# Spatial gates: the first tile's z projection ahead of its u projection, and the block inverse's conversions in their written order on ScalarE

## The chip, the cores and the metric

The kernel runs on one core of a Trainium2 chip. A core has five engines that run side by side: TensorE (PE in the profile; its weight loads are PEld) for matmuls, VectorE (DVE), ScalarE (ACT) and GpSimd (POOL) for elementwise work, and SyncE (SP), which here only issues DMAs. ACT and POOL issue DMAs too. Each engine takes its instructions in the order in which they were queued; an instruction waits on semaphores for its inputs, and what is queued behind it waits as well.

The metric is the device time of one execution in microseconds. The kernel before takes 2145.91 us, the median of 3 runs (2145.07 to 2146.69).

## The reference

One layer of a backbone with three parallel token mixers, for 2048 sample tokens and 128 prompt tokens of width 1024:

```python
proj = jnp.einsum('btd,de->bte', xn, w_in)
qkv, beta, dec, z_a, u_b, v_b, z_b, x_c, z_c, gates = jnp.split(proj, points, axis=-1)
...
o, s_f, s_b = delta_bidir(q, k, v, g, beta, s0_f, s0_b)
o_a = (rmsnorm(o, o_norm_g) * jax.nn.silu(z_a)).reshape(B, T, W_BR)
o_b = chunk_sgu(u_b, v_b, sgu_norm_g, w_spatial, b_spatial) * jax.nn.silu(z_b)
o_c = fourier_mix(x_c, grid) * jax.nn.silu(z_c)
br = jnp.stack([o_a, o_b, o_c], axis=2)
pb = jnp.einsum('btnw,nwd->btnd', br, w_branch)
merged = jnp.einsum('btnd,btnd->btd', jax.nn.sigmoid(gates), pb)
return jnp.einsum('btd,de->bte', merged, w_out), s_f, s_b
```

Two parts matter here. `chunk_sgu` (branch B) normalizes v, mixes it over the 128 tokens of a chunk by `w_spatial`, giving vs, and multiplies u by it; the result is gated by silu(z). `delta_bidir` (branch A) is a gated delta rule: in each chunk of tokens a triangular system with a unit diagonal is solved, then a state is carried from chunk to chunk, forwards and backwards.

## The kernel before

The 2176 tokens lie along the free dimension as five tiles, `TBS`: four of 512 and one of 128. Every matmul operand is a pair of float16 tiles, a high and a low part, so a product of a weight block (8 contraction steps) with a tile of 512 tokens is 24 matmuls: high by high, high by low, low by high for each step (`gemm_T`, and the matmul itself is on line 250). A conversion of an array into such a pair is always an activation on ScalarE that writes the high part and an instruction on VectorE that subtracts it and writes the low part.

The program has a main line and a generator, `delta`, which is branch A's work. The main line runs the projections one after another: v for all 17 chunks (`spatial` mixes a chunk's v and makes `vs`, L1498; `vstore` writes it to DRAM, L1504), then the spatial gates (the loop `for g in range(4)` with tiles `ti` in it), then the Fourier branch, then the merges. After each product it calls `pace.tick(us)`, which takes one `weight_step` (a piece of the conversion of a later weight block: square on L315, scale, high part L327, low part L328) and advances `delta` by a step for each 1.6 us of its argument. The order in which all this is written gives the priorities.

The order on each engine is then made at build time: a planner runs through a simulated time and gives each engine the instruction of the best priority among those whose inputs it takes to be there. `tc.high_priority()` lifts an instruction above others. `tc.issue_after(ins)` forbids one to be queued ahead of `ins` on the same engine; it is no wait for its end. `queued()` of the wrapper `_InTurn` is that for the newest instruction written so far on the engine. On the chip the order is fixed.

*Spatial gates.* For each of the four column groups g the row `vrow` of vs is read back from DRAM into SBUF: for g = 0 in five pieces by SP (L1542), for later g in one read during the group before (L1548). For a tile, u is multiplied (24 matmuls into a PSUM bank of `ps_mm`, which has three), and L1554 on VectorE, of high priority, writes u times vs into `vrow`. Then `gate_unit` calls `silu_unit`: z is multiplied into another bank, ACT makes the sigmoid (L1454), VectorE z times it (L1456), both of high priority. `gate_unit` goes on with the product of the two on GpSimd (L1466), its squares on ACT (L1467) and the store to DRAM from GpSimd (L1468). `silu_unit` can also be called earlier and its result handed to `gate_unit` as `sg`; the Fourier branch does so for three tiles. In that case `gate_unit`'s own tick is 0.2 us and not that of a product.

*Branch A beside it.* `prep` prepares one chunk: TensorE transposes rows of k and q (L1016), ACT squares them (L1022), VectorE and GpSimd make the norms (L1023, L1024), VectorE writes `tok` (L1033), TensorE transposes it (L1049), ACT and VectorE make the pair `T` (L1050, L1051), products of T with itself follow (L1064 to L1069) and with q (L1080 to L1083). `late` issues the stores from ACT, one stage behind. `base_inverse` runs between the stages of `prep`, one step of it for each: for a group of up to four chunks it reads the blocks `nd` into the one buffer `XB` (L1103), turns a half of them (L1107), and in 31 rounds of a VectorE product (L1114) and a GpSimd subtraction (L1115) makes the inverse E. Then four conversions of E into `XB`, each of one activation (L1122) and one VectorE instruction (L1123), with a yield behind each, and stores of the result, which `late` issues from ACT (L1003) in the next stages. `XB` is read again for the next group when these stores have landed. When all chunks are done the last group's inverse runs, and then `scan`, which needs the results.

Of the kernel before, what the change touches and what calls it, by code (L numbers as in the profile page):

```python
# [14 lines left out]
AF = mybir.ActivationFunctionType  # L15
# [20 lines left out]
FS = 4096.0  # L36
# [158 lines left out]
def hybrid_flow_kernel(ctx: ExitStack, tc: tile.TileContext, x_prompt, x_sample, state_delta, c, c_ctx, w_ada,  # L195
# [4 lines left out]
    G, V, A, PE = [_InTurn(tc, e_) for e_ in (nc.gpsimd, nc.vector, nc.scalar, nc.tensor)]  # L200
    uid, rot = [0], [0]

    def nm(s):
        uid[0] += 1
        return f"{s}_{uid[0]}"
# [4 lines left out]
    def sb(pl, shape, tag, dt=F32, bufs=None):  # L210
        kw = {} if bufs is None else {"bufs": bufs}
        return pl.tile(list(shape), dt, tag=tag, name=nm(tag), **kw)
# [11 lines left out]
    def bank(pl, shape, tag="b"):  # L224
        if pl is ps_d:
            rot[0] += 1
            pl = ps_d[rot[0] % 3]
        return pl.tile(list(shape), F32, tag=tag, name=nm(tag))
# [110 lines left out]
    def gemm_T(ps, w, c0, rh, rl, nkt=KT, start=True, stop=True):  # L339
        for k in range(nkt):  # L340
            mm(ps, w.hi[:, k, c0:c0 + P], rh[:, k, :], start and k == 0, False)
            mm(ps, w.hi[:, k, c0:c0 + P], rl[:, k, :], False, False)
            mm(ps, w.lo[:, k, c0:c0 + P], rh[:, k, :], False, stop and k == nkt - 1)
            if k % 2:
                pace.part(rh.shape[-1] / 400)
# [57 lines left out]
    def getw(n=1, ahead=0):  # L403
        i = wnext[0]
        wnext[0] += n
        fetch(i + n)
        while len(wdone) - len(wsteps) < i + n:
            weight_step()
        fetch(i + n + ahead)
        r = wdone[i:i + n]  # L410
        return r[0] if n == 1 else r
# [34 lines left out]
    pace = Pace()  # L446
# [257 lines left out]
    for ti, (t0, tn) in enumerate(TBS):  # L704
        g = 0 if t0 < NS else 1
# [225 lines left out]
    for ct in range(12):  # L931
        w = getw(1, 2 if ct < 6 else min(4, 15 - ct))
# [159 lines left out]
    def base_inverse(g):  # L1092
        nt = len(GROUPS[g])
        nb = 16 * nt
        XB = sb(dq, [P, 2048], "XB")
        X, tmp = XB[:, 0:1024], XB[:, 1024:2048]
        E = sb(dq, [P, 1024], "E")
        if nt < 4:
            V.memset(X, 0.0)
            V.memset(tmp, 0.0)  # L1100
        b3 = lambda t_: t_.rearrange("p (j i) -> p j i", j=32)
        for d in range(2):
            SY.dma_start((X if d == 0 else tmp)[64 * d:64 * d + nb, :], ndD[g][d].rearrange("t h (b j) i -> (t h b) (j i)", b=4))  # L1103
        for _ in range(8):
            yield 0
        with V.queued():
            V.tensor_copy(b3(X[64:P, :]), tmp[64:P, :].rearrange("p (i j) -> p j i", j=32))  # L1107
        G.memset(E, 0.0)
        G.memset(E[:, 0:1024:33], 1.0)
        X3, E3 = b3(X), b3(E)  # L1110
        for k in range(31, 0, -1):
            n_ = 32 - k
            t3 = tmp[:, 0:k * n_].rearrange("p (j i) -> p j i", j=k)
            V.tensor_tensor(t3, X3[:, 0:k, k:k + 1].to_broadcast([P, k, n_]), E3[:, k:k + 1, k:32].to_broadcast([P, k, n_]), ALU.mult)  # L1114
            G.tensor_tensor(E3[:, 0:k, k:32], E3[:, 0:k, k:32], t3, ALU.subtract)  # L1115
            if k % 2 == 0:
                yield 1
        both = XB.bitcast(F16).rearrange("p (j l w c) -> p j l w c", j=32, l=2, w=2)
        for j0 in (0, 16):
            js = slice(j0, j0 + 16)  # L1120
            for w, src in ((0, E3), (1, E.rearrange("p (i j) -> p j i", j=32))):
                A.activation(both[:, js, 0, w, :], src[:, js], AF.Copy, scale=FS)  # L1122
                V.scalar_tensor_tensor(both[:, js, 1, w, :], src[:, js], FS, both[:, js, 0, w, :], ALU.mult, ALU.subtract)  # L1123
                yield 1
            out = [(eD[g][d][js].rearrange("j t (y x) -> (t y) j x", x=128),
                    both[64 * d:64 * d + nb, js].rearrange("p j l w c -> p j (l w c)")) for d in range(2)]
            if g < 4:
                extra.extend(out)
            else:
                SY.dma_start(*out[0])  # L1130
                A.dma_start(*out[1])
# [278 lines left out]
    def delta():  # L1410
# [5 lines left out]
        for i_, (g, ci, t) in enumerate(seq):  # L1416
            if ci == 0 and g:
                for r_ in base:
                    if r_:
                        yield 1  # L1420
                base = base_inverse(g - 1)
            for n_, _ in enumerate(prep(g, ci, t, seq[i_ + 1][2] if i_ < 16 else None, held)):
                yield 1
                if next(base, 0):
                    yield 1
# [6 lines left out]
        for _ in base_inverse(4):  # L1432
            yield 1
# [14 lines left out]
    def silu_unit(ti, w, out_scale=None):  # L1448
        t0, tn = TBS[ti]
        ps = bank(ps_mm, [P, tn])  # L1450
        gemm_T(ps, w, 0, xh[:, :, t0:t0 + tn], xl[:, :, t0:t0 + tn])
        sg = sb(ep, [P, tn], "sg", bufs=4)
        with tc.high_priority():
            A.activation(sg, ps, AF.Sigmoid, scale=w.inv)  # L1454
        with tc.high_priority():
            V.scalar_tensor_tensor(sg, ps, w.inv if out_scale is None else out_scale, sg, ALU.mult, ALU.mult)  # L1456
        return sg

    def gate_unit(n, g, ti, w, src, sg=None, out_scale=None):

        t0, tn = TBS[ti]
        own = sg is None
        if own:
            sg = silu_unit(ti, w, out_scale)
        o = sb(ep, [P, tn], "st", bufs=3)
        G.tensor_tensor(o, sg, src, ALU.mult)  # L1466
        A.activation(sg, o, AF.Square, accum_out=oss[n][:, g * 5 + ti:g * 5 + ti + 1])  # L1467
        G.dma_start(obD[n][g, :, t0:t0 + tn], o)  # L1468
        pace.tick(tn / 100 if own else 0.2)
# [73 lines left out]
    for g in range(4):  # L1543
        uw, zw = getw(2, 2)
        vrow = vnext
        if g < 3:
            vnext = sb(vp, [P, NTOK], "vrow")
            SY.dma_start(vnext, vsD[g + 1])  # L1548
        for ti, (t0, tn) in enumerate(TBS):
            st = vrow[:, t0:t0 + tn]  # L1550
            ps = bank(ps_mm, [P, tn])
            gemm_T(ps, uw, 0, xh[:, :, t0:t0 + tn], xl[:, :, t0:t0 + tn])
            with tc.high_priority():
                V.scalar_tensor_tensor(st, ps, uw.inv, st, ALU.mult, ALU.mult)  # L1554
            pace.tick(tn / 100)
            gate_unit(1, g, ti, zw, st)

    vst.close()

# [18 lines left out]
    for g in range(4):  # L1578
        xw, zw = getw(2, 2)
# [611 lines left out]
```

## Time and profile before

| what | before |
| --- | --- |
| median of 3 runs | 2145.91 us |
| the profiled execution's own time | 2150.07 us |
| its span in the profile | 2148.3 us |
| mean granted TensorE clock | 0.992 |
| busy: TensorE, VectorE, ScalarE, GpSimd | 2085.2, 1327.9, 1060.8, 843.3 us |
| L1554, u times vs | 20 times, 13.3 us |
| L1454, sigmoid of the gates of both branches | 40 times, 24.8 us |
| L1456 in the spatial gates | 20 times, 13.3 us |
| L1122, high parts of the inverse | 20 times, 15.6 us |
| L1123, low parts of the inverse | 20 times, 18.1 us |
| HBM traffic | 186 GB/s over the span |

A line of the profile's order of time reads: start in us, duration, engine, line of the kernel, operation, output and inputs with their shapes, how many in a row, and in brackets how long the engine sat idle before and what ended that. A matmul of 512 columns is shown with 0.38 us, but the next begins 0.215 us later, since they are pipelined. The granted clock is a share of the full speed. An idle time that is put down to one releaser can have had another: the profile names the input that came last by its records.

### The profile page before, as it was taken

The numbers are of one execution on the slowest core, as the hardware profiler recorded it, in microseconds if no ns is written. First come the engines' busy times: TensorE is split into PE (matmuls) and PEld (weight loads), VectorE is DVE, ScalarE is ACT, GpSimd is POOL, SyncE is SP. The second block draws the span as 40 slices with busy tenths as digits, with TensorE's granted clock in tenths as the row PEclk, the third lists the DMA queues.
The fourth block names the chain that finished last, engine by engine and source line by source line (L and its number), as shares of the span: only waits on it lengthen the run. The fifth ranks groups of instructions, "written<-read, shape, count | busy, mean of one in ns | idle before, by whom it ended". The sixth has DMA issues, their size and how long they took to land.

```text
span 2148.3 us, 42630 instructions
## 1 busy us (share of the span) xinstructions
PE 2085.2 (97%) x16133; PEld 1196.8 (56%) x16133; DVE 1327.9 (62%) x2945; ACT 1060.8 (49%) x2457; POOL 843.3 (39%) x1089
## 2 busy tenths in 40 slices
PE   7999999999999999989899999999999999999997
PEld 4454444455555677777555556565655444444443
DVE  6656854388777786456655555766665564666245
ACT  5554744475656664445544445665653353453112
POOL 0321332225565555542321233354542234333464
PEclk9999999999999999999999999999999999999999
DMA  9525722277877743444655555867664655456852
GB/s 353 219 77 189 267 102 102 74 223 226 259 228 246 225 138 93 121 132 138 205 182 161 167 162 184 258 206 232 210 204 127 209 167 173 167 198 240 335 220 89
DMA packets 222910, 403.25 MB, mean 188 GB/s; under 512 B 39720, under 2 KB 109632, under 8 KB 219888
## 3 DMA queue, kind: packets, MB, share of 16 engines
q1 hardware_dynamic: 167664, 290.84, 42.5%
q0 software_dynamic: 15216, 65.89, 8.2%
q10 hardware_dynamic: 39824, 43.79, 6.0%
q8 instruction: 127, 2.08, 0.4%
q14 instruction: 79, 0.65, 0.1%
HBM read 258.19 MB, written 142.24 MB: 186 GB/s over the span
## 4 chain that ended last, share of the span: by engine, by line
PE 70%; DVE 9%; DMA 9%; ACT 4%; POOL 4%; issue 3%; SPq 1%; ACTq 0%; DVEq 0%; POOLq 0%
PE b L250 66%; PE b L182 4%; DMA st<-br 2%; POOL E L1115 1%; DMA pa<-pa 1%; DMA wst<-in_w_blk_dram 1%; DVE XB L1114 1%; POOL st L1466 1%; DMA ab<-in_w_adb_dram 1%; PE b L1016 1%; DMA sqk<-qk 1%; DMA ei<-XB 0%; ACT xh L182 0%; ACT nd L1066 0%; DVE XB L1123 0%
## 5 line engine op out<-in xcount | busy, mean ns | idle before, releaser
L250 PE MATMUL b<-xh,whi 128*128 128x512 f16 (+1 forms) x1920 | 651.1, 348 | 2.8 <-DVE sg L1456 1.8
L250 PE MATMUL b<-xl,whi 128*128 128x512 f16 (+1 forms) x1920 | 651.2, 348 | 0.0
L250 PE MATMUL b<-xh,wlo 128*128 128x512 f16 (+1 forms) x1920 | 650.1, 347 | 0.0
L250 PEld LDWEIGHTS <-whi 128*128 128x128 f16 x3856 | 352.7, 98 | 326.4 <-issue 7.3
L250 PEld LDWEIGHTS <-wlo 128*128 128x128 f16 x1928 | 188.8, 98 | 176.1 <-issue 2.2
L250 PE MATMUL b<-big,bhi 128*128 128x512 f16 (+1 forms) x960 | 252.3, 347 | 1.9 <-ACT big L1699 1.1
L250 PE MATMUL b<-big,blo 128*128 128x512 f16 (+1 forms) x480 | 163.1, 347 | 0.0
L1743 POOL TENSOR_TENSOR mrow<-mrow,sg 128x512 f32<-128x512 f32 (+1 forms) x80 | 94.4, 1182 | 131.2 <-DVE sg L1742 99.5
L953 POOL TENSOR_TENSOR cy<-cy,raw 128x545 f32<-128x545 f32 (+1 forms) x48 | 65.8, 1395 | 181.8 <-ACT raw L952 181.8
L250 PEld LDWEIGHTS <-xh 128*128 128x128 f16 x1496 | 116.9, 98 | 28.8 <-issue 1.4
L250 PEld LDWEIGHTS <-bhi 128*128 128x128 f16 x960 | 87.7, 98 | 78.1 <-issue 2.6
L1115 POOL TENSOR_TENSOR E<-E,XB 128x31 f32<-128x31 f32 (+15 forms) x155 | 94.1, 607 | 85.7 <-DVE XB L1114 68.8
L250 PEld LDWEIGHTS <-xl 128*128 128x128 f16 x1068 | 98.1, 98 | 44.8 <-DMA tw<-tw 1.4
L1733 ACT ACTIVATE sg<-b,winv 128x512 f32<-128x512 f32 (+1 forms) x120 | 73.9, 616 | 87.1 <-PE b L250 86.4
L1188 POOL COPY T<-ES 32x256 f16<-32x256 f16 x68 | 31.8, 467 | 188.6 <-DMA ES<-ei 167.9
L250 PE MATMUL b<-whi,xh 128*128 128x128 f16 x544 | 92.8, 219 | 0.0
L250 PE MATMUL b<-whi,xl 128*128 128x128 f16 x544 | 92.8, 219 | 0.0
L250 PE MATMUL b<-wlo,xh 128*128 128x128 f16 x544 | 92.8, 219 | 0.0
L328 DVE SCALAR_TENSOR_TENSOR wlo<-wst,wsc,whi 128x1024 f16<-128x1024 f32 x52 | 71.1, 1368 | 33.1 <-ACT whi L327 32.7
L315 ACT ACTIVATE wlo<-wst 128x1024 f16<-128x1024 f32 x52 | 54.9, 1055 | 54.5 <-DMA wst<-in_w_blk_dram 51.2
L1114 DVE TENSOR_TENSOR XB<-XB,E 128x31 f32<-128x31 f32 (+15 forms) x155 | 55.2, 356 | 41.8 <-POOL E L1115 41.2
L1295 POOL TENSOR_TENSOR skn<-skn,ed 128x512 f32<-128x512 f32 x34 | 37.7, 1109 | 109.7 <-DMA skn<-kv 109.7
(532 smaller groups left out, 4317.9 us busy)
## 6 DMA issues: line engine op xcount, KB each, us to landing
wst<-in_w_blk_dram SPq DMA_DIRECT2D x58, 512.0 KB, 4.5
pa<-pa POOLq DMA_DIRECT2D x16, 896.0 KB, 4.4
qkv<-cy POOLq DMA_DIRECT2D x12, 1089.0 KB, 5.3
st<-br SPq DMA_DIRECT2D x48, 256.0 KB, 3.2
mrow<-mrg SPq DMA_DIRECT2D x16, 576.0 KB, 4.6
pa<-pa SPq DMA_DIRECT2D x5, 1792.0 KB, 17.3
dc<-dec SPq DMA_DIRECT2D x17, 512.0 KB, 4.8
kq<-qkv SPq DMA_DIRECT2D x34, 256.0 KB, 4.5
```

The costliest lines, as they stand in the source:

```text
L182: self.last = f(*args, **kw)
L250: newest[0] = PE.matmul(out, l, r, start=start, stop=stop, skip_group_check=reopened)
L315: w.squared = A.activation(w.lo, st, AF.Square, accum_out=ss)
L328: w.low = V.scalar_tensor_tensor(w.lo, st, s, w.hi, ALU.mult, ALU.subtract)
L953: G.tensor_tensor(y[:, c0:c1], y[:, c0:c1], raw[:, 1 + c0:1 + c1], ALU.mult)
L1016: PE.transpose(ps[:, hs(h)], cur[part][:, h, :], ident)
L1114: V.tensor_tensor(t3, X3[:, 0:k, k:k + 1].to_broadcast([P, k, n_]), E3[:, k:k + 1, k:32].to_broadcast([P, k, n_]), ALU.mult)
L1115: G.tensor_tensor(E3[:, 0:k, k:32], E3[:, 0:k, k:32], t3, ALU.subtract)
L1188: G.tensor_copy(T16[rows(a0, b), :, :, b], ES[0:32, :, 2 * a0 + b, :, wT])
L1295: G.tensor_tensor(h3(kn_), h3(kn_), bc(ed[:, d, t, :], P), ALU.mult)
L1733: gated_[0] = A.activation(sg, ps, AF.Sigmoid, scale=gw.inv)
L1743: G.tensor_tensor(mr, mr, sg, ALU.add)
```

## The change

Two edits. In the spatial gates, for the first tile of the first group alone, z is multiplied, its sigmoid taken and a tick made before u is multiplied; `gate_unit` gets the result and makes its short tick. The tile so has three ticks and not two: 5.12, 5.12 and 0.2 us. In the block inverse each of the four high-part activations may no longer be queued on ScalarE ahead of the newest instruction that was written for ScalarE before it.

```diff
             for w, src in ((0, E3), (1, E.rearrange("p (i j) -> p j i", j=32))):
-                A.activation(both[:, js, 0, w, :], src[:, js], AF.Copy, scale=FS)
+                with A.queued():
+                    A.activation(both[:, js, 0, w, :], src[:, js], AF.Copy, scale=FS)
                 V.scalar_tensor_tensor(both[:, js, 1, w, :], src[:, js], FS, both[:, js, 0, w, :], ALU.mult, ALU.subtract)
                 yield 1
...
             st = vrow[:, t0:t0 + tn]
+            front = None
+            if (g, ti) == (0, 0):
+                front = silu_unit(ti, zw)
+                pace.tick(tn / 100)
             ps = bank(ps_mm, [P, tn])
             gemm_T(ps, uw, 0, xh[:, :, t0:t0 + tn], xl[:, :, t0:t0 + tn])
             with tc.high_priority():
                 V.scalar_tensor_tensor(st, ps, uw.inv, st, ALU.mult, ALU.mult)
             pace.tick(tn / 100)
-            gate_unit(1, g, ti, zw, st)
+            gate_unit(1, g, ti, zw, st, front)
```

## The prediction

> **What bounds the kernel now.** First the head of the page and its chain of waits: which engine is full, and what the end hangs on.
>
> ```profile
> span 2148.3 us, 42630 instructions
> PE 2085.2 (97%) x16133; PEld 1196.8 (56%) x16133; DVE 1327.9 (62%) x2945; ACT 1060.8 (49%) x2457; POOL 843.3 (39%) x1089
> ...
> PE 70%; DVE 9%; DMA 9%; ACT 4%; POOL 4%; issue 3%; SPq 1%; ACTq 0%; DVEq 0%; POOLq 0%
> ```
>
> TensorE is busy for 2085.2 of 2148.3 us. Neither edit takes a matmul away, so nothing can be won but idle time of TensorE, 63.1 us in the whole span. Second, the busy time by stretch, to see how much of it lies where the diff works. The columns are the stretch and its length, busy time with instruction counts of TensorE, of its weight loads, of DVE, ACT and POOL, then the granted clock, the DMA share and GB/s.
>
> ```profile
> 541.00:575.00 34.00, 31.61 (x180) 16.32 (x179) 23.24 (x52) 19.59 (x63) 15.77 (x25) 1.00 0.87 286
> 575.00:640.00 65.00, 63.23 (x441) 36.45 (x439) 50.53 (x114) 40.02 (x123) 43.92 (x62) 1.00 0.70 222
> 640.00:750.00 110.00, 110.00 (x830) 66.51 (x829) 79.38 (x182) 68.08 (x209) 61.68 (x88) 1.00 0.74 236
> ...
> 890.00:930.00 40.00, 33.58 (x345) 22.81 (x343) 16.25 (x41) 15.02 (x36) 20.00 (x34) 0.87 0.45 134
> ```
>
> The spatial gates run from about 527 to 750 us. Their start leaves TensorE idle for 34.00 - 31.61 = 2.39 us, the next 65 us for 1.77 us, the rest for nothing. The gap of 890 to 930 us (6.42 us, and a clock of 0.87) is where the scan begins. Third, the order of time around the first tile, engine by engine: start, duration, engine, line, operation, and in brackets the idle time before it with what ended it. ACTq and SPq are the DMA issues of ACT and SP.
>
> ```profile
> 541.59 1.12 DVE L1498 SCALAR_TENSOR_TENSOR vs<-b,vg,bsp 128x128 f32<-128x128 f32 x4
> ...
> 542.74 0.38 ACTq L1504 DMA_DIRECT2D vs<-vs  x1
> ...
> 543.16 0.69 ACT L1454 ACTIVATE sg<-b,winv 128x512 f32<-128x512 f32 x1 [4.29 <-DVE wsc L278]
> ...
> 543.88 0.75 DVE L1456 SCALAR_TENSOR_TENSOR sg<-b,winv,sg 128x512 f32<-128x512 f32 x1
> ...
> 546.76 1.04 POOL L1024 TENSOR_TENSOR ss<-ss,mhalf 128x4 f32<-128x4 f32 x1
> ...
> 547.56 0.17 DVE L1023 TENSOR_SCALAR ss<-ss 128x4 f32<-128x4 f32 x1 [0.53 <-ACT sq L1022]
> ...
> 548.57 2.23 SPq L1542 DMA_DIRECT2D vrow<-vs  x5
> ...
> 551.17 0.75 DVE L1554 SCALAR_TENSOR_TENSOR vrow<-b,winv,vrow 128x512 f32<-128x512 f32 x1 [3.44 <-DMA vrow<-vs]
> ...
> 551.83 0.68 DVE L1033 TENSOR_TENSOR tok<-b,ss 128x512 f32<-128x512 f32 x1
> ...
> 552.43 2.39 DVE L1123 SCALAR_TENSOR_TENSOR XB<-E,XB 128x512 f16<-128x512 f32 x2
> ...
> 552.66 0.63 PE L1049 MATMUL b<-cst,tok 128*128 128x128 f32 x4 [1.85 <-DVE tok L1033]
> ...
> 557.43 0.60 ACT L1050 ACTIVATE T<-b 128x512 f16<-128x512 f32 x1 [3.36 <-DVE XB L1123]
> ...
> 558.81 0.77 PE L250 MATMUL b<-T 128*128 128x128 f16 x11 [0.17 <-DVE T L1051]
> ...
> 569.34 0.63 PE L1049 MATMUL b<-cst,tok 128*128 128x128 f32 x4 [0.33 <-DVE tok L1033]
> ...
> 586.78 0.38 PE L250 MATMUL b<-xh,whi 128*128 128x512 f16 x1 [1.77 <-DVE sg L1456]
> ```
>
> The first tile's u product (L1554) needs vrow, which goes through DRAM: DVE ends the last vs at 542.71, ACT stores it from 542.74, SP can start reading it back only at 548.57, and DVE gets it at 551.17. DVE takes its queue in order, so it idles 3.44 us before L1554. Behind it stands L1033, whose own input was there when L1024 ended, at 546.76 + 1.04 = 547.80. TensorE stands in its turn before the transposes L1049 of tok, 1.85 us. That wait, 0.17 and 0.33 us make 2.35 of the 2.39 us.
>
> **The change, part by part. First, z ahead of u.** The 24 matmuls of each product are the same and only change places. They end here, the first row the last of the first product and the second that of the second:
>
> ```profile
> 533.69 0.38 PE L250 MATMUL b<-xh,wlo 128*128 128x512 f16 x1
> ...
> 540.21 0.38 PE L250 MATMUL b<-xh,wlo 128*128 128x512 f16 x1
> ```
>
> So z is complete at about 534.1 instead of 540.6 us, and u at 540.6 instead of 534.1. The u product has to wait for vrow until 551.17 either way, so being 6.5 us later costs it nothing: 551.17 - 540.6 leaves 10.6 us of cover. Its PSUM bank was held until 551.9 before, and that stays; z's bank was free at 544.6 and is free earlier.
>
> What moves is the sigmoid (0.69) on ACT and its product (0.75) on DVE. They leave the places at 543.16 and 543.88 and enter at about 534 to 536, among the work that makes the last vs:
>
> ```profile
> 534.22 0.63 ACT L1068 ACTIVATE n<-n 128x512 f16<-128x512 f32 x1
> 534.75 0.71 ACT L1527 ACTIVATE st<-sg,vss 128x512 f16<-128x512 f32 x1
> ...
> 535.65 1.07 DVE L1528 SCALAR_TENSOR_TENSOR st<-sg,vss,st 128x512 f16<-128x512 f32 x1
> ...
> 541.35 0.32 DVE L1114 TENSOR_TENSOR XB<-XB,E 128x156 f32<-128x156 f32 x1 [0.42 <-POOL E L1115]
> ```
>
> Ends of the effect on vs: 0, if the sigmoid fits behind L1527 and DVE's idle 0.42 us before 541.35 takes the rest; 0.69 + 0.75 = 1.44 us, if both stand in the chain L1527, L1528, spatial matmuls, L1498. I take 0.7, since ACT's row at 534.22 starts at once when z is ready and one of the two engines has to give way. On the other side L1033's inputs come up to 0.69 us sooner, because the sigmoid no longer stands ahead of the squares that feed L1023.
>
> The order on DVE is chosen at build time by when inputs are expected. L1554 went in front of L1033 inside a narrow slot: after L1023 at 547.56, and L1033 was ready at 547.80. Moving vrow 0.7 us later and tok up to 0.7 us sooner is more than that slot, so I expect L1033 in front. Then it runs at about 547.8, ready for transposes that TensorE wants at 552.66 - 1.85 = 550.8; the 1.85 us go, and with L1050 no longer behind the late L1123 also the 0.17 and 0.33. What is late next is L1554 at about 551.9, and behind it u's bank, which the third tile's u product wants only at 554.64, where its first matmul stands:
>
> ```profile
> 554.64 0.38 PE L250 MATMUL b<-xh,whi 128*128 128x512 f16 x1
> ```
>
> 2.7 us of cover less L1554's 0.75 leaves about 2. If that cover goes, each us later is a us of TensorE.
>
> The tile also gets a third, short tick. It gives the weight conversion one step more, earlier by a tile, and the delta stage 0.2 us of pace. The pieces of such a step are here:
>
> ```profile
> 543.75 1.14 ACT L327 ACTIVATE whi<-wst,wsc 128x1024 f16<-128x1024 f32 x1
> ...
> 544.92 1.38 DVE L328 SCALAR_TENSOR_TENSOR wlo<-wst,wsc,whi 128x1024 f16<-128x1024 f32 x1
> ```
>
> Bounds: nothing where ACT idles (4.29 us at 543.16), or 1.38 us of DVE ahead of L1033; even that leaves it inside the 3.0 us from 547.80 to 550.8, so I take 0. A weight read issued sooner stands behind the vrow reads on SP, which blocks until 548.57 anyway. The gate's product, square and store on POOL and ACT still follow u and are not moved past anything.
>
> **Second, the conversions L1122 behind the newest ACT instruction.** It adds no instruction, only an order, for 20 activations. Where they stood before:
>
> ```profile
> 537.74 1.14 ACT L1082 ACTIVATE n<-n 128x512 f16<-128x512 f32 x2
> ...
> 548.06 3.09 ACT L1122 ACTIVATE XB<-E 128x512 f16<-128x512 f32 x4 [0.53 <-POOL E L1115]
> ...
> 721.68 1.61 ACT L1122 ACTIVATE XB<-E 128x512 f16<-128x512 f32 x2
> 723.20 0.71 ACT L1041 ACTIVATE q<-qr,qsc 128x512 f16<-128x512 f32 x1
> 723.81 0.61 ACT L1082 ACTIVATE n<-n 128x512 f16<-128x512 f32 x1
> ...
> 879.00 3.12 ACT L1122 ACTIVATE XB<-E 128x512 f16<-128x512 f32 x4
> ```
>
> By the text the four of a group are interleaved with the L1068 and L1082 of one chunk. At 548 us that chunk's last L1082 had ended 9 us before (537.74 + 1.14), so the new edge binds nothing; at 879 no chunk is left, and they wait for the inverse alone. At 722 the fourth ran ahead of the L1082 written before it; it falls back by one or two instructions, 0.6 to 1.2 us, with TensorE never idle between 640 and 750. Ends: 0.6 us sooner for L1082, 1.2 us later for the conversion; on the path 0. The cover is that full TensorE; without it 1.2 us.
>
> **Sum.** -1.85 - 0.17 - 0.33 = -2.35 us on the profiled execution, whose own time is 2150.07 us (span 2148.3 and 1.8 around it). That run lies 4.2 us over the median of the runs, 2145.91; the difference carries over: 2145.91 - 2.35 = 2143.6 us. Own bounds: 0.3 us won, if only half of the 0.17 and 0.33 goes and tok is still late by the 1.38 us, up to 4.1 (with the 1.77 us at 586.78).
>
> **The rivals.** *The gain runs on to the scan.* L1123, 552.43 now, could run at about 549; the inverse's buffer is read out and refilled sooner, and ACT's queue, which the 3.36 us blocked, runs ahead, so the 1.77 us at 586.78 go as well. If the scan's first loads also come 3 us sooner, half of the 6.42 us goes: -2.35 - 1.77 - 3.2 = -7.3, 2138.6 us. For it: those waits are on the inverse's output. Against it: the refill is tied to the next chunk's T conversion in each of the later groups, which follows TensorE.
>
> *Slower: L1554 stays in front, and vrow comes later.* Place: DVE at 551. Price: 1.44 us more wait before L1049, 1.85 + 1.44 = 3.29 us. If a wait of that length drops the clock as in the stretch of 890 to 930, whose longest single wait is shorter, 40 x 0.13 = 5.2 us come on top: +6.6, 2152.5 us. It decides once DVE's order is unchanged and the wait passes about 2.5 us:
>
> ```profile
> PE b L250 <- DMA ES<-ei: 3.6, 2, 2.5
> ...
> PE b L250 <- DMA N<-n: 1.9, 1, 1.9
> ```
>
> For it: high priority of L1554, and the sigmoid ahead of L1527. Against it: 541 to 575 kept a clock of 1.00 through 1.85 us. [...]
>
> *The order stays and the clock holds:* +1.4 or less, 2145.9 to 2147.3; the second edit alone does nothing, which is what its rows say.
>
> **How the numbers follow.** Forecast 0.34, gain to the scan 0.27, slower 0.31, no effect 0.08. The order of all that follows, 2148.3 - 575 = 1573 us, is planned anew, so each case is blurred by some us. A measurement of this kernel tells 0.2% (4.3 us) from no change. Faster by more: 0.27 and a third of the forecast, 0.11, so 0.38. Within: the forecast's other 0.23 and 0.08, so 0.31. Slower: 0.31. The range takes in both outer cases and a little beyond for the blur: 2137 to 2153; the forecast's own is 2141.8 to 2145.6.
>
> **What would show it.** Right: in the new order of time L1033 starts before L1554, L1049 has no wait at about 550, the idle time of 541 to 575 is below 0.5 us, and L1454 stands near 535. Wrong: L1554 still in front; a clock under 1.00 there; L1122 pulled apart by more than 5 us with the refill later; or the stretches after 750 changing by more than these two did, which would mean the new planning, not the edits themselves, made the time.

## The result and the profile after

The changed kernel takes 2163.36 us, the median of 4 runs (2158.18 to 2164.75); the kernel before, run beside it, takes 2145.55 us (4 runs, 2145.07 to 2146.69). The ratio is 1.008, with a 95% interval of 1.0062 to 1.0097: 17.8 us slower by the medians, and above the predicted range, which ended at 2153. In e6, e9 and e12 below, one execution of 3642 to 3880 us at a granted clock of 0.56 to 0.71 is left out of the median.

The head of the page of the changed kernel:

```profile
span 2156.4 us, 42659 instructions
PE 2086.0 (97%) x16133; PEld 1197.4 (56%) x16133; DVE 1327.3 (62%) x2945; ACT 1062.5 (49%) x2457; POOL 842.8 (39%) x1089
```

TensorE is busy 2086.0 us, as before (2085.2). So the loss in the profile is nearly all idle time: 2156.4 - 2086.0 = 70.4 us instead of 63.1, which is 7.3 of the 8.1 us that the span grew by. This one execution took 2158.18 us, the fastest of its four, while the profiled execution of before, 2150.07, lies above all four of its kernel. The pair of profiles therefore shows 8.1 of the 17.8 us. The busy time by stretch of the changed kernel, columns as in the prediction:

```profile
541.00:575.00 34.00, 31.06 (x170) 15.56 (x169) 20.70 (x48) 18.38 (x61) 15.20 (x25) 1.00 0.89 276
...
890.00:930.00 40.00, 32.94 (x347) 23.60 (x345) 17.37 (x42) 17.02 (x39) 20.20 (x34) 0.83 0.50 146
1400.00:1560.00 160.00, 158.41 (x1393) 94.13 (x1394) 91.93 (x237) 90.62 (x263) 75.62 (x95) 0.99 0.66 203
1560.00:1600.00 40.00, 34.89 (x291) 19.66 (x290) 24.51 (x63) 19.26 (x52) 15.91 (x19) 0.96 0.59 188
```

And two stretches of the kernel before that the prediction did not look at:

```profile
1400.00:1560.00 160.00, 159.74 (x1466) 96.89 (x1465) 100.25 (x251) 96.43 (x278) 80.67 (x101) 1.00 0.70 217
1560.00:1600.00 40.00, 38.73 (x368) 23.82 (x367) 27.60 (x72) 21.20 (x61) 17.60 (x21) 1.00 0.63 190
```

Idle time of TensorE by stretch, worked out as length less busy time:

| stretch, us | what runs there | before | after |
| --- | --- | --- | --- |
| 0 to 541 | projections, v and vs | 15.88 | 14.70 |
| 541 to 750 | spatial gates | 4.16 | 5.31 |
| 750 to 960 | last inverse, start of the scan | 14.25 | 13.39 |
| 960 to 1400 | Fourier branch, first merge | 12.65 | 15.00 |
| 1400 to 1560 | second merge | 0.26 | 1.59 |
| 1560 to 1600 | second merge | 1.27 | 5.11 |
| 1600 to 2000 | end of the second, third merge | 2.30 | 1.15 |
| 2000 to 2110 | output product | 0.26 | 2.06 |
| 2110 to the end | end of the output product | 12.10 | 12.06 |

In the spatial gates, 541 to 750, idle time grew by 1.2 us instead of falling by 2.4. How much of such a step is scatter can be read from e7, e13, e14, e16 and e17 below, which differ from the kernel before only from the scan on: they idle 3.08 to 4.40 us there, and 1.93 to 2.61 us in 541 to 575. The changed kernel's 5.31 us and 2.94 us lie above that by less than 1 us. So it is clear that the gain is missing, and the small loss is hardly more than scatter. The largest single step, 3.8 us at 1560 to 1600, lies a thousand microseconds behind the first tile and some 700 behind the last group of conversions.

**At the first tile.** The order of time of the changed kernel. Its lines from L1123 on stand one further down than before, those behind the gates five: L1559 is the u product of L1554, L1468 the gate's square of L1467, L1455 the sigmoid.

```profile
535.41 0.67 ACT L1455 ACTIVATE sg<-b,winv 128x512 f32<-128x512 f32 x1
...
544.43 0.69 DVE L1033 TENSOR_TENSOR tok<-b,ss 128x512 f32<-128x512 f32 x1 [1.00 <-POOL ss L1024]
...
546.77 0.60 PE L1049 MATMUL b<-cst,tok 128*128 128x128 f32 x4
...
549.75 0.75 DVE L1559 SCALAR_TENSOR_TENSOR vrow<-b,winv,vrow 128x512 f32<-128x512 f32 x1 [3.11 <-DMA vrow<-vs]
...
551.94 0.63 ACT L1468 ACTIVATE sg<-st 128x512 f32<-128x512 f32 x1 [6.21 <-POOL st L1467]
...
552.57 2.10 ACT L1123 ACTIVATE XB<-E 128x512 f16<-128x512 f32 x3
...
554.57 0.58 ACT L1050 ACTIVATE T<-b 128x512 f16<-128x512 f32 x1
...
555.21 0.23 PE L250 MATMUL b<-T 128*128 128x128 f16 x1 [1.79 <-ACT T L1050]
```

The sigmoid moved to 535, L1033 runs in front of L1559, and L1049 starts with no wait: those steps came as predicted. But now ScalarE stands still, 6.21 us, before L1468, the square of the gate's product, which needs u and so vrow. Behind it in ScalarE's queue are the inverse's conversions and L1050, which makes T. TensorE, no longer late for tok, is late for T by 1.79 us. In the kernel before, the same square came behind the conversions:

```profile
553.35 0.63 ACT L1467 ACTIVATE sg<-st 128x512 f32<-128x512 f32 x1 [2.20 <-POOL st L1466]
```

There it waited 2.20 us at 553, after the four conversions of 548.06. With z earlier, the planner put the square ahead of them. The wait for vrow did not go away. VectorE still stands 3.11 us for it before L1559 (3.44 before), and now ScalarE stands for its result as well.

**In the second merge.** ScalarE, TensorE and SP of the changed kernel near 1587 us; L315 is the square of a weight block (wlo, wst), L1738 the merge's sigmoid, L1219 and L1232 conversions of the scan, L291 the read of a weight block and L1782 that of rows of `w_ada`:

```profile
1578.26 0.63 ACT L1232 ACTIVATE u<-sv 128x512 f16<-128x512 f32 x1 [0.69 <-PE b L250]
1587.10 1.06 ACT L315 ACTIVATE wlo<-wst 128x1024 f16<-128x1024 f32 x1 [8.21 <-DMA wst<-in_w_blk_dram]
...
1588.28 0.69 ACT L1738 ACTIVATE sg<-b,winv 128x512 f32<-128x512 f32 x1
1588.86 0.36 ACT L1219 ACTIVATE Q<-b 64x256 f16<-64x256 f32 x1
```

```profile
1583.82 0.77 PE L250 MATMUL b<-u,kn 128*128 128x128 f16 x11 [1.95 <-DVE u L1233]
...
1589.94 0.33 PE L250 MATMUL b<-R,Q 128*128 128x64 f16 x6 [1.46 <-DVE Q L1220]
```

```profile
1572.62 0.40 SPq L1782 DMA_DIRECT2D wst<-in_w_ada_dram  x1
...
1582.16 0.35 SPq L291 DMA_DIRECT2D wst<-in_w_blk_dram  x1
```

And VectorE there:

```profile
1579.71 2.42 DVE L476 SCALAR_TENSOR_TENSOR sg<-wst,scT,sg 128x256 f32<-128x256 f32 x3
...
1583.09 0.68 DVE L1233 SCALAR_TENSOR_TENSOR u<-sv,u 128x512 f16<-128x512 f32 x1
1588.28 0.16 DVE L264 CAST wscb<-wss 128x1 bf16<-128x1 f32 x1 [4.52 <-ACT wlo L315]
```

The square waits 8.21 us for its read. The read was issued late, at 1582.16, because the rows of `w_ada` hold one of the two `wst` buffers until VectorE has added them up (L476); in the list of SP's waits the read stands with 5.8 us for it. TensorE first waits 1.95 us for u, whose low part (L1233) stands behind these sums, and then for what ScalarE has queued behind the square: 1.46 us for Q, 1.21 for S and 0.48 for the scaled o. That is the whole 5.1 us of the stretch: 1.95 us of it belong to the sums on VectorE, 3.15 to what stands behind the square. VectorE stands behind the square too: L264, which needs the square's result, keeps it idle for 4.52 us, and the next S and the low part of Q come behind it. In the kernel before the read was no earlier, and the square still waited, but less stood behind it:

```profile
1582.72 0.70 ACT L1733 ACTIVATE sg<-b,winv 128x512 f32<-128x512 f32 x1
1583.29 0.38 ACT L1218 ACTIVATE Q<-b 64x256 f16<-64x256 f32 x1
...
1588.73 1.06 ACT L315 ACTIVATE wlo<-wst 128x1024 f16<-128x1024 f32 x1 [3.55 <-DMA wst<-in_w_blk_dram]
```

```profile
1583.79 0.38 SPq L291 DMA_DIRECT2D wst<-in_w_blk_dram  x1
```

The sigmoid and the conversion of Q, here at 1582.7 and 1583.3, are what in the changed kernel stands behind the square.

### The profile page after: what moved, and what is told of

Its sections match the earlier page's. It is cut to its first block, busy times and chain, and to the rows that moved or that the text cites. A ratio compares the mean times of both kernels' runs of the same rounds, so it can differ in the third digit from the quotient of the medians.

```text
span 2156.4 us, 42659 instructions
## 1 busy us (share of the span) xinstructions
PE 2086.0 (97%) x16133; PEld 1197.4 (56%) x16133; DVE 1327.3 (62%) x2945; ACT 1062.5 (49%) x2457; POOL 842.8 (39%) x1089
## 4 chain that ended last, share of the span: by engine, by line
PE 49%; DMA 6%; DVE 5%; POOL 2%; ACT 2%; issue 2%; SPq 1%; ACTq 0%; POOLq 0%; DVEq 0%
PE b L250 48%; DMA st<-br 2%; DMA wst<-in_w_blk_dram 1%; DMA tw<-tw 1%; DMA ES<-ei 1%; DMA ei<-XB 0%; POOL E L1115 0%; POOL st L1467 0%; PE b L1383 0%; DVE XB L1114 0%; DVE big L1705 0%; ACT nd L1066 0%; DVE xh L182 0%; ACT big L1704 0%; DVE wlo L328 0%
## 5 line engine op out<-in xcount | busy, mean ns | idle before, releaser
L1738 ACT ACTIVATE sg<-b,winv 128x512 f32<-128x512 f32 (+1 forms) x120 | 74.1, 617 | 93.3 <-PE b L250 92.6
L315 ACT ACTIVATE wlo<-wst 128x1024 f16<-128x1024 f32 x52 | 54.9, 1056 | 65.8 <-DMA wst<-in_w_blk_dram 62.3
L327 ACT ACTIVATE whi<-wst,wsc 128x1024 f16<-128x1024 f32 x52 | 59.3, 1142 | 35.3 <-DVE wsc L278 35.1
```

The costliest lines, as they stand in the source:

```text
L315: w.squared = A.activation(w.lo, st, AF.Square, accum_out=ss)
L327: w.made = A.activation(w.hi, st, AF.Copy, scale=s)
L1738: gated_[0] = A.activation(sg, ps, AF.Sigmoid, scale=gw.inv)
```

## Experiments

Each kernel ran beside the kernel before on the same chip. The difference is that of the medians in the same table row. The interval need not have the ratio of these medians at its middle.

| label | edit | median, us | before, us | difference | ratio, 95% |
| --- | --- | --- | --- | --- | --- |
| e1 | first edit alone | 2158.33 | 2145.19 | +13.1 | 1.0034 to 1.0066 |
| e2 | second edit alone | 2150.39 | 2145.19 | +5.2 | 1.0014 to 1.0035 |
| e3 | 0.2 us of pace at the gate alone | 2155.24 | 2145.19 | +10.0 | 1.0029 to 1.0052 |
| e4 | both edits, no third tick | 2151.63 | 2145.19 | +6.4 | 1.0015 to 1.0040 |
| e5 | exchange of z and u alone | 2146.80 | 2146.99 | -0.2 | 0.9989 to 1.0013 |
| e6 | one weight step more at the gate alone | 2144.42 | 2146.99 | -2.6 | 0.9982 to 1.0002 |
| e7 | 0.2 us of pace ahead of the merges alone | 2153.64 | 2146.99 | +6.7 | 1.0024 to 1.0055 |
| e8 | 0.2 us of pace less at the gate | 2149.62 | 2146.99 | +2.6 | 0.9998 to 1.0031 |
| e9 | second edit, last group alone | 2147.17 | 2146.39 | +0.8 | 0.9978 to 1.0010 |
| e10 | second edit, groups before the last | 2151.48 | 2146.39 | +5.1 | 1.0004 to 1.0032 |
| e11 | e3 with the merges' reads asked for earlier | 2156.20 | 2146.39 | +9.8 | 1.0025 to 1.0051 |
| e12 | these reads alone | 2146.58 | 2146.39 | +0.2 | 0.9987 to 1.0012 |
| e13 | rows of `w_ada` in the last merge only | 2148.72 | 2146.28 | +2.4 | 0.9998 to 1.0030 |
| e14 | e13 with the pace of e7 | 2152.30 | 2146.28 | +6.0 | 1.0019 to 1.0043 |
| e15 | e13 with the whole change | 2160.84 | 2146.28 | +14.6 | 1.0046 to 1.0094 |
| e16 | squares behind the scaling of o | 2162.62 | 2147.66 | +15.0 | 1.0046 to 1.0108 |
| e17 | e16 with the pace of e7 | 2152.26 | 2147.66 | +4.6 | 1.0007 to 1.0039 |
| e18 | e16 with the whole change | 2157.59 | 2147.66 | +9.9 | 1.0030 to 1.0061 |

### Which part costs (e1 to e6)

e1 and e2 are the change's two hunks, one each. e4 and e5 take the short tick out of the first tile:

```diff
-        pace.tick(tn / 100 if own else 0.2)
+        if (n, g, ti) != (1, 0, 0):
+            pace.tick(tn / 100 if own else 0.2)
```

e3 and e6 are the kernel before with one half of such a tick behind the first gate (`weight_step()` in e6):

```diff
             gate_unit(1, g, ti, zw, st)
+            if (g, ti) == (0, 0):
+                pace.steps(0.2)
```

> Only the first edit (z ahead of u, with its third tick); the conversions are as before. Theory A, the loss is made at the first tile, where the conversions stand behind the gate's square L1468 and hold up T: without the second edit the wait of 1.79 us for T is gone, 541 to 575 us idles under 1 us, and the time is 2143 to 2145 us. Theory B, the loss is made far behind, by the new tick's 0.2 us of pace, which moves later steps of the delta stage to other ticks: the time stays within 5 us of the changed kernel's 2163 us.

> Only the second edit (the conversions behind the newest ScalarE instruction). Theory A: it does harm only together with the first, 2145 to 2148 us. Theory B: no tick is changed, so the steps stay with their ticks, 2144 to 2148 us. A third theory C, the second edit alone does it, by putting off the refill of XB in every group: 2155 us or more, with the inverses' ends some us later in each group.

> The kernel before, with 0.2 us more pace given to the delta stage behind the first tile of the spatial gates, and nothing else: no order of z and u, no edge, no step of weights. Theory A: nothing near the first tile changes, 2144 to 2148 us. Theory B: the same steps are moved to other ticks as by the change, so most of its loss is here, 2155 to 2166 us, and the stretches from 1000 us on idle more than before.

> Both edits, but the first tile's gate makes no third tick, so that ticks, pace and weight steps are as before. Theory A: as slow as the changed kernel, 2158 to 2165 us, with the wait for T of about 1.8 us. Theory B: within 4 us of the kernel before, 2142 to 2150 us, though the wait for T is there.

> Only the exchange of z and u on the first tile: no third tick, no new place for the conversions. Theory B (loss by pace) and the prediction's own step: L1033 stands ahead of L1554, the wait of 1.85 us before L1049 is gone, and the time is 0 to 3 us under the kernel before, 2142 to 2146 us. Theory A (loss at the first tile): 2150 us or more.

> The kernel before with one step of weight conversion more behind the first tile and no pace. Theory B: the conversion only comes earlier by a tile where ScalarE has room, 2144 to 2147 us, and the idle time of ScalarE before L315 stays at 54 to 56 us. If the weight step is half of the tick's harm: 2150 us or more.

Measured: the exchange alone does nothing (-0.2 us), nor does the weight step (-2.6 us, its interval reaches past none). The second edit costs 5.2 us. The 0.2 us of pace cost 10.0 us alone, and with both edits in place the tick costs 17.8 - 6.4 = 11.4 us, taken from two comparisons. The parts alone add up to -0.2 - 2.6 + 10.0 + 5.2 = 12.4 us of 17.8, so they do not quite add. Theory B named the right part in e1 and e3. Two forecasts missed: e2 at 2150.39 us lies between all three of its theories, and e4, 6.4 us above the kernel before, fits neither of its own; the 5.2 us of the second edit are most of it.

In e5 the exchange is seen without the tick and without the second edit. ScalarE, then TensorE, of e5:

```profile
553.29 0.63 ACT L1467 ACTIVATE sg<-st 128x512 f32<-128x512 f32 x1 [6.24 <-POOL st L1466]
...
553.92 3.09 ACT L1122 ACTIVATE XB<-E 128x512 f16<-128x512 f32 x4
```

```profile
557.54 0.23 PE L250 MATMUL b<-T 128*128 128x128 f16 x1 [2.37 <-ACT T L1050]
```

The square is ahead of the conversions here too, and the wait for T is 2.37 us against the 1.85 us for tok that went. The exchange gains what it was to gain and gives it back about 9 us later.

### The pace (e7, e8)

A tick's argument is added to an account, and each 1.6 us in it buys a step of branch A (1.3 us once the scan runs). An extra 0.2 us is never taken back: from there on one step in six to eight is written one call earlier. e7 gives it where the merges begin, e8 takes 0.2 us away at the gate:

```diff
+    pace.steps(0.2)
     inv_ = merge(1, True, inv_, then=(2, 20))
```

> The kernel before with the 0.2 us of pace given only at the start of the merges, when the scan has begun. Theory B in the form that the harm is made in the scan, where its steps come to stand behind a weight's square L315 that waits for its read: 2151 to 2160 us, ScalarE's idle time before L315 at 60 us or more, and the waits at L1382 near 1400 us as with the pace given early. If the harm is made between 750 and 1080 us: 2144 to 2148 us.

> The kernel before with 0.2 us less pace from the first tile on. Theory B as a matter of direction (steps that come earlier meet a read that is late): no loss, 2140 to 2147 us. Theory B as a matter of any other phase (the order before is a good one among many): slower by 5 us or more, 2150 us and above.

Given only at the merges, the pace still costs 6.7 us, with nothing changed ahead of them. Less pace at the gate does not win: 2.6 us slower, an interval that just reaches none, and a time between its two theories. The stretch of 1560 to 1600 us of e7:

```profile
1560.00:1600.00 40.00, 34.80 (x291) 19.58 (x290) 24.23 (x63) 18.79 (x51) 15.73 (x19) 0.96 0.60 187
```

40 - 34.80 = 5.20 us idle, as in the changed kernel (5.11), so the loss near 1587 us comes with the pace and needs neither edit. The further 3.3 us of e3 (10.0 less 6.7) were not traced, and the intervals of the two runs leave it open whether they are there.

### The second edit by group (e9, e10)

```diff
-                A.activation(both[:, js, 0, w, :], src[:, js], AF.Copy, scale=FS)
+                with (A.queued() if g == 4 else ExitStack()):
+                    A.activation(both[:, js, 0, w, :], src[:, js], AF.Copy, scale=FS)
```

e10 has `g < 4` in that place.

> The kernel before, with the second edit for the last group of the block inverse alone (g == 4). Theory 1: the 5.2 us that the whole second edit costs come from the last group, whose four conversions ran in one piece (879.00, 3.12 us) and come apart to 886.0 us in the build that has the edit for all groups, so that the scan begins 2 to 4 us later: then this kernel loses 3 to 6 us (2148 to 2152 beside a before of 2145 to 2147), with most of it as idle time of TensorE between 880 and 960 us. Theory 2: the loss comes from the earlier groups, or from the order of everything behind that the build plans anew: then this kernel is within 2 us of before.

> The kernel before, with the second edit for the groups before the last alone (g < 4). Theory 1 (the last group makes the loss): within 2 us of before. Theory 2 (the earlier groups, or the new planning): 3 to 6 us slower than before, and the idle time of TensorE is spread over 800 to 960 us as in the kernel with the edit for all groups. If both this kernel and the one for the last group lose 4 to 6 us, the two do not add, and any shift of the order in this place has such a price.

The loss sits in the groups before the last (e10 +5.1, e9 +0.8 us), so the first theory, that the last group delays the scan, falls. The first, the fourth and the last group of e10, and the read of the last group's blocks:

```profile
548.90 2.13 ACT L1123 ACTIVATE XB<-E 128x512 f16<-128x512 f32 x3 [0.53 <-POOL E L1115]
...
556.10 1.10 ACT L1123 ACTIVATE XB<-E 128x512 f16<-128x512 f32 x1 [1.13 <-DVE XB L1124]
...
811.02 1.15 ACT L1123 ACTIVATE XB<-E 128x512 f16<-128x512 f32 x2
...
822.42 1.07 ACT L1123 ACTIVATE XB<-E 128x512 f16<-128x512 f32 x1
...
879.68 3.11 ACT L1123 ACTIVATE XB<-E 128x512 f16<-128x512 f32 x4
```

```profile
830.73 1.15 SPq L1103 DMA_DIRECT2D XB<-nd  x2
```

The fourth group and that read in the kernel before:

```profile
817.61 3.11 ACT L1122 ACTIVATE XB<-E 128x512 f16<-128x512 f32 x4
```

```profile
828.64 1.13 SPq L1103 DMA_DIRECT2D XB<-nd  x2
```

Four conversions that ran in one piece come apart, and the buffer is refilled 2.1 us later for the last group. The loss is not simply that: the last group's conversions start at 879.68 instead of 879.00, and kernels with the same order up to there start them anywhere from 878.15 (e17) to 879.41 us (e7), so 0.7 us is within their scatter of 1.3. Nor does the profile of e10 show the loss as idle time: TensorE idles 60.7 us of its span of 2149.3 us, where it idled 63.1 of 2148.3 before, and is busy 3.4 us longer. With the edit in all groups, 800 to 960 us idles 14.5 us in e2 and 14.7 in e4 (10.57 before), but 11.44 in e10 and 10.66 in the changed kernel. So no one place holds the cost, and what makes the 5 us stays open.

### The reads (e11, e12)

```diff
-                wlate[0] = 2
+                wlate[0] = 2 if gated_[0] is None else 1
```

> The kernel before with 0.2 us more pace at the first gate (which cost 10.0 us alone), and in the merges each weight block's read is asked for one weight step earlier than before. Theory 1: the 10 us come from the weight's square on ScalarE that waits 3.4 us and 7.6 us for its read, in front of the scan's scaling of o: then with earlier reads the square's idle time, 62.1 us in the pace kernel, falls below 50 us, TensorE's waits at the transposes of o fall below 1 us, and the time comes within 3 us of the next kernel (same reads, no pace). Rival: the pace costs by the new planning of the whole order, whatever the reads do: then this kernel stays 7 to 12 us slower than the next.

> The control for the kernel above: the kernel before with the reads of the merges' weights asked for one step earlier and no pace. Theory 1: the weight's square waits less than the 54.5 us of before, TensorE's few waits there were not on it, so the time is 2143 to 2148 us. Rival: this also plans the order behind it anew, and can fall 5 us or more to either side.

The edit did not do what it was for: in e11 the square near 1586 us still waits 7.9 us, since what holds the read is a buffer and not the moment it is asked for. The squares that write wlo wait 64.6 us in all in e11 and 49.7 in e12, and e12 is no faster than before (54.5 us there). So the sum of these waits says nothing about the time. The rival had the difference of the two right (7 to 12 us; 2156.20 - 2146.58 = 9.6), but since the read stayed late, the pair left the cause open.

### Taking the rows of `w_ada` away (e13 to e15)

```diff
-                if each is not None and (n == 0 or db > 3):
+                if each is not None and n == 0:
                     next(gates, 0)
```

The rows are read and added up in the last merge only.

> The kernel before, with the rows of w_ada (L1777), which take one of the two wst buffers between the weight blocks, read in the last merge only and not already in the second. It is the control for the next two. Both theories: the read of the block at about 1583 us no longer waits for L476, TensorE's 1.3 us of idle time at 1593 may go, 2143 to 2148 us. More than 2150 would say that the last merge cannot take these reads.

> The same, with 0.2 us of pace given just ahead of the merges, which cost 6.7 us where the rows were read in the second merge (2153.64 beside 2146.99). Theory 1: 5.6 us of that are the square's 8.3 us wait near 1587 us, with the scan's conversions and the gate's sigmoid queued behind it on ScalarE, and the wait is there because the read waits for the buffer; then TensorE's idle time of 1560 to 1600 us falls from 5.2 to below 1.5 us, and this kernel is at most 3 us slower than the control. Theory 2: the new order costs as a whole, and another wait takes the place of that one: 5 to 9 us slower than the control.

> The same, with the whole change, which cost 17.8 us. Theory 1: the 5.5 us of that one stretch go, and with it a part of what the pace costs: 8 to 13 us slower than the control, 2153 to 2159. Theory 2: 15 us or more slower than the control, 2160 to 2166. If it came within 4 us of the control, all of the change's loss would hang on these reads, which the loss of the second edit, 5.2 us, speaks against.

The same stretches of e14, and its square:

```profile
1400.00:1560.00 160.00, 155.83 (x1381) 93.11 (x1382) 91.18 (x237) 89.82 (x256) 75.47 (x95) 0.99 0.63 201
1560.00:1600.00 40.00, 40.00 (x364) 24.01 (x363) 22.98 (x60) 22.72 (x65) 19.43 (x27) 1.00 0.65 198
```

```profile
1578.87 1.06 ACT L315 ACTIVATE wlo<-wst 128x1024 f16<-128x1024 f32 x1 [2.35 <-DMA wst<-in_w_blk_dram]
```

The read is no longer held, the square waits 2.35 us instead of 8.31 (e7), and TensorE's 5.20 us idle in 1560 to 1600 are gone. Beside its control e13 the pace now costs 2152.30 - 2148.72 = 3.6 us instead of 6.7, and the whole change 2160.84 - 2148.72 = 12.1 us instead of 17.8: 5.7 us less, about what the stretch showed. Both lie where theory 1 had them or just beside (at most 3 us, 8 to 13 us). The intervals of the times are wide, some 3 us to either side; the stretch is the stronger evidence. The held buffer and the sums on VectorE were taken away together and not apart. The control itself is no gain (2148.72, just above its forecast): 1560 to 1600 us idles 0.13 us instead of 1.27, but 1700 to 2000, where the rows are read now, 4.74 instead of 1.96.

What remains of e14's 3.6 us shows in the first stretch: 160 - 155.83 = 4.17 us idle, 4.0 of them before one transpose of o near 1403, behind a square again. The last three kernels go there.

### Every square behind the scaling of o (e16 to e18)

```diff
-        with behind_gate():
+        with behind_gate(), (ExitStack() if scaled_[0] is None else tc.issue_after(scaled_[0].ins)):
             w.squared = A.activation(w.lo, st, AF.Square, accum_out=ss)
...
-            A.activation(o[:, hs(h)], o[:, hs(h)], AF.Copy, scale=ss[:, h:h + 1])
+            scaled_[0] = A.activation(o[:, hs(h)], o[:, hs(h)], AF.Copy, scale=ss[:, h:h + 1])
```

> The kernel before, with each weight square L315 of the merges queued behind the newest scaling of o (L1378) instead of wherever it fell. It is the control for the next two, and a change that could help by itself: before has 1.3 us of TensorE's idle time in 1400 to 1700 us that such squares could make. Theory 1: 2142 to 2147 us. Theory 2: the order behind is planned anew, up to 5 us to either side.

> The same with 0.2 us of pace given just ahead of the merges, which cost 6.7 us without the new place of the squares. Theory 1: all of that is the squares in front of the scan's conversions, at 1400 and at 1587 us; then TensorE's idle time of 1400 to 1700 us falls from 8.2 to below 3 us, its waits at the transposes of o fall below 1.5 us, and this kernel is at most 3 us slower than the control. Theory 2 (the order as a whole): 5 to 9 us slower than the control.

> The same with the whole change. Theory 1: of the 17.8 us the pace's part in the merges, 7 to 10 us, goes, and the second edit's 5 us and some of the stretches ahead of the merges stay: 6 to 11 us slower than the control. Theory 2: 14 us or more slower than the control.

Nothing of this was foreseen. Without the pace the edit costs 15.0 us, outside of what both theories allowed; with the pace the kernel is 2162.62 - 2152.26 = 10.4 us faster than without. The list of TensorE's waits from 1080 to 1720 us, of e16 and then of e17 (us in total, times, longest):

```profile
PE b L1383 <- ACT o L1379: 6.3, 5, 1.5
PE b L251 <- DVE sg L1743: 4.4, 2, 3.2
```

```profile
PE b L251 <- DVE sg L1743: 3.1, 2, 1.8
PE b L251 <- DMA of<-sz: 2.8, 1, 2.8
```

e17 has no wait left for the scaled o, as theory 1 said of it; e16 has five. But e17's idle time of 1400 to 1700 us is 5.1 us and not below 3, so theory 1 is half right. e16 idles 4.03 us in 1400 to 1560 and 6.97 in 1600 to 1700 (0.26 and 0.34 before): its squares are where they were meant to be, and other waits came. That e17 is no more than 3 us slower than its control comes out formally, by a control that became slow. So 0.2 us of pace have no price of their own. They cost 10.0 us in one order of ScalarE's queue and win 10.4 in another. e18 fits neither of its theories: it is 5.0 us faster than its control. e16, e17 and e18 have wide intervals, 3 to 7 us to either side, which 10.4 us exceeds and 5.0 us does not.

No kernel of the study beats the kernel before by more than the measurement can tell; e6 comes nearest.

## Why the prediction was wrong

**The exchange: order right, gain lost.** "L1033 in front" came true, and the wait of 1.85 us before L1049 went. The sigmoid and its product did go in, at 535 and 537 us, and vs was later by about 0.5 us in e5 (0.7 taken). What failed is the sentence that the gate's product, square and store "still follow u and are not moved past anything". The square does follow u, but on ScalarE it was moved ahead of four conversions and of L1050, with 6.2 us of waiting. The prediction asked what is late next on VectorE and for the PSUM bank; both held. It did not ask it for ScalarE, the third engine that works for the same tile. -2.35 us became -0.2 by time (e5); the stretch of 541 to 575 idles 2.60 us in e5 and 2.94 in the changed kernel, not below 0.5. The lower bound of 0.3 us was also a wrong sum: 1.85 - 1.38 + 0.25 is 0.7.

**The third tick: taken as 0, measured about 10.** This is the step that failed by most. The prediction priced its pieces where they run, around 544 us, and saw them covered; the weight step half of it was indeed worth nothing (e6). The other half, 0.2 us of pace, was named and not priced (10.0 us in e3, 6.7 in e7). It issues nothing at the gate; it shifts every later step of branch A by an eighth to a sixth of a step against the main line. At 1587 us, the one place that was traced to its cause, that decided whether the merge's sigmoid and the scan's conversions stand ahead of or behind a square that waits 8.2 us. That wait was in the trace of before, with 3.55 us at 1588.73, and could have been listed as a place at which any shift of the scan has a price.

**The second edit: taken as 0, measured 5.2.** "By the text the four of a group are interleaved with the L1068 and L1082 of one chunk" was the error. By the text of the kernel, the newest ScalarE instruction when a conversion is written can also be one of the main line, since `delta` only runs inside a tick, or a store issued from ScalarE. At 548 us, where the prediction said that the edge "binds nothing", the fourth conversion ran behind the gate's square and a store of the inverse's first half, at 556.10 in e10. At 722 it was right that only one falls back, by 2.7 us in e10 and not 0.6 to 1.2. At 879, where only the inverse was to count, e9 has the last two conversions 1.8 us behind the first two, which cost nothing that the times show (+0.8). Which of these places makes the 5.2 us stays open.

**The rivals.** "L1554 stays in front" named a price for the slower side, but its mechanism did not happen: the order did change. The blur of "some us" for the new planning was the right worry, with a size far too small: e8 to e18 lie between +0.2 and +15.0 us from edits that move a few instructions by a few places. The stated sign for it, stretches behind 750 us changing by more than the first ones, is what the trace shows (table above). Half of another sign came too: the changed kernel's fourth group of conversions runs from 809.72 to 821.54 us instead of 3.11 us in one piece, though its buffer is read again no later (828.74, before 828.64).

## What to carry to other kernels

Before a step is costed at nothing, ask what is issued behind it on every engine that works for the same tile, and look for instructions that stand in an in-order queue in front of others and wait on a DMA (here the square L315, which waited 8.21 us for its read near 1587 us): at that square the shift far upstream was paid for. An argument that is a share of an account, such as a pace, is not priced by its size; it re-deals an order, and the honest estimate is the spread that such re-deals have shown, here about 15 us of 2146. A sum of waits on an engine off the critical path (49.7 to 65 us here) does not rank kernels; what stands behind each wait does.

## What the runs showed of the hardware

The granted clock of 1395 to 1408 us was 0.87 after single waits of 2.62 us (the changed kernel) and 2.73 us (e3), as the prediction's slower rival feared with its point of about 2.5 us. TensorE of the changed kernel near 1401 us, first the wait, then matmuls of 512 columns:

```profile
1400.94 0.33 PE L1383 MATMUL b<-cst,o 128*128 128x128 f32 x1 [2.62 <-ACT o L1379]
...
1402.25 0.63 PE L250 MATMUL b<-xh,whi 128*128 128x512 f16 x1
1402.68 0.63 PE L250 MATMUL b<-xl,whi 128*128 128x512 f16 x1
```

They are 0.43 us apart instead of 0.215, from 1401.1 to 1404.6 us (3.0 to 3.3 us long in e1, e3 and e14), and the granted clock of 1401 to 1405 is 0.57. The same place in e15 has a wait of almost the same length, and no drop; its row of the stretch 1395 to 1408 follows:

```profile
1405.04 0.33 PE L1383 MATMUL b<-cst,o 128*128 128x128 f32 x1 [2.55 <-ACT o L1379]
```

```profile
1395.00:1408.00 13.00, 10.45 (x96) 6.14 (x94) 7.33 (x22) 7.46 (x17) 7.00 (x10) 1.00 0.73 226
```

Over seven kernels, waits of 2.62 (the changed kernel), 2.73 (e3), 3.38 (e1) and 4.00 us (e14) at that place go with a clock of 0.87 in 1395 to 1408, and waits of 2.29 (e11), 2.33 (e7) and 2.55 us (e15) with 1.00.

The length of one wait does not settle it. Near 1593 us in the changed kernel matmuls are 0.43 us apart again, until 1595.6, and no wait in the 9 us before them is longer than 1.46 us:

```profile
1592.79 0.48 PE L1383 MATMUL b<-cst,o 128*128 128x128 f32 x1 [0.48 <-ACT o L1379]
1593.06 0.63 PE L250 MATMUL b<-xh,wlo 128*128 128x512 f16 x1
1593.48 0.63 PE L250 MATMUL b<-xh,whi 128*128 128x512 f16 x1
```

There the waits of 1.46, 1.21 and 0.48 us stand close together, from 1588 to 1592 us TensorE is busy for 1.33 of 4.00 us, and the granted clock of 1592 to 1596 is 0.57, as in 1401 to 1405. What of this made the clock fall, no run here tests. By an estimate from the 3.5 us in which matmuls begin 0.43 us apart instead of 0.215, such a drop costs about half of them, 1.7 us, on top of the wait.
